# A second ring of weight places for the late modulation, its shares in two stages, and x1 read from PSUM

## The chip, the core and the metric

One core of one Trainium2 chip runs the kernel. The metric is the device time of one execution in microseconds (us); smaller is better. The engines are named as in the profile: PE is TensorE (matrix products; PEld is its weight load), DVE is VectorE, ACT is ScalarE, POOL is GpSimd, and SP is SyncE, whose queue issues nearly all transfers from HBM.

## The reference

One layer of a hybrid diffusion backbone on 256 latent tokens and 256 context tokens of width 2048, all in float32. Cut to what matters here:

```python
sh1, sc1, g1, sh2, sc2, g2 = jnp.split(jax.nn.silu(c) @ w_ada[l] + b_ada[l], 6, axis=-1)
p = modulate(rmsnorm(x, norm_mix[l]), sh1, sc1) @ w_in[l]        # split into the columns of both branches and the gates
y_mla_l = attend_latent(q_l, k_l, v_l, k_c, v_c)                  # latent attention, 8 heads
o_dn_l, _ = dn_bidirectional(lq, lk, lv, lgd, lbeta, s_ctx, True) # gated delta rule, two directions, from the context's state
merged = jax.nn.sigmoid(gate_mla) * (y_mla @ w_o_mla) + jax.nn.sigmoid(gate_dn) * (y_dn @ w_o_dn)
x = x + g1 * (merged @ w_out)                                     # x1
h = modulate(rmsnorm(x, norm_ffn[l]), sh2, sc2)
gate, val = jnp.split(h @ w_up, 2, axis=-1)
x = x + g2 * ((jax.nn.silu(dwconv_centred(gate, conv_w)) * val) @ w_down)
```

## The kernel before, in words

Activations lie with channels on the 128 partitions and the 256 tokens (T) along the row. Every large product is made from two halves: a weight block is loaded in float32 (`raw`, 128x1024, 512 KB), ScalarE casts it to the high half (`whi`, L120), VectorE subtracts to get the low half (`wlo`, L121), and TensorE multiplies both (`mm_hl`, L68): a 128x512 product with the high half, whose two halves of 256 columns hold the activation's high and low part, and a 128x256 product with the low half. One output tile is therefore in one PSUM bank as two halves of 256 columns that still have to be added: `gather` does this with a copy on ScalarE (L513) and an add on VectorE (L514).

`raw` has a ring of NR = 5 places (pool `wr`, tag "raw"); `whi` and `wlo` have NH = 6 each. SP, ACT and VectorE run in the order in which the program is written; TensorE does so in the attention and in the scan, elsewhere a scheduler orders it. A load whose place is still in use holds up what is behind it on SP.

The stages, with where they lie in the profiled span: projections and attention to about 730 us; the scan of the gated delta rule (`scan`, tiles `S`, `r`, `kp`, `yp`, `o`) from about 735, whose gaps on TensorE are filled by other tiles (`e_fill`): gate projections `wgd` (`gtp`, copied to `zx`) and the attention branch's output projection `womla` (`brp`, `ox`, `t1`); the norm of o; the delta branch's projection `wodn`; the output projection `wout` (`ops`, from about 995), whose loop over f makes x1 and its sum of squares; the norm; the FFN (`fps`, 1100 to 1590), whose first four tiles are made k by k while `h2_tile` makes h and H; the down projection (`dps`).

The late modulation is `ada_rest`: the last four of the six modulation vectors (g1, sh2, sc2, g2; one value for each of 128 x 64 channels) are made on VectorE, not on TensorE. 128 loads of 512 KB (`rawa`, L259) are each multiplied by the row of silu(c) (`sch`, 128x1024, reloaded from `Sc` for each half) and summed in one instruction (a "dot", L278, followed by a small read of the sum into `parts`). It is a generator: `ada(c)` adds c to what is owed, and a dot pays 1300. So ADS (in the scan, times the cost the scan reports), the number 1 (a dot for each of the scan's last pieces) and WO (each wout tile) set how many dots stand where. Its loads used the same five places as the weights, and one load was issued ahead of the dot before it. g1 must be done before x1, sh2 and sc2 before the norm's end, g2 before the down projection.

```python
x1[:, f] = yx * adaT[:, f] + xr      # L1387, yx = ops high half + low half
```

Of the kernel before, what the change touches and what calls it, by code (L numbers as in the profile page):

```python
# [8 lines left out]
F32 = mybir.dt.float32  # L9
F32R = mybir.dt.float32r  # L10
AF = mybir.ActivationFunctionType
ALU = mybir.AluOpType
# [4 lines left out]
P = 128  # L17
D = 2048
KD = D // P
T = 256  # L20
# [7 lines left out]
GR = 1024  # L28
GH = 512
NR = 5  # L30
# [6 lines left out]
CB = 3000  # L37
CC = 7000
RE = 1.0
ADS = 0.3  # L40
OD = 8000
OC = 4000
WO = 1500
IK = 7000
NW = 4
SCP = (0, 2, 4, 6)
# [7 lines left out]
def hybrid_block(ctx: ExitStack, tc: tile.TileContext, io, dbg=None):  # L54
    nc = tc.nc
    act, dve, pool, sync = nc.scalar, nc.vector, nc.gpsimd, nc.sync
# [23 lines left out]
    def pool_(name, bufs, side="left"):  # L80
        return tc.tile_pool(name=name, bufs=bufs, side=side, reuse_waits="tile")
# [4 lines left out]
    wr = ctx.enter_context(pool_("wr", 2))  # L86
# [4 lines left out]
    def dump(name, ap):  # L91
        if dbg is not None and name in dbg:
            sync.dma_start(dbg[name], ap)
# [8 lines left out]
    half = const.tile([P, 1], F32, name="half")  # L102
# [26 lines left out]
    def load_w(src):  # L129

        g = []
        for o in range(0, src.shape[1], GR):
            raw = raw_w(src[:, o : min(o + GR, src.shape[1])])
            for i in range(0, raw.shape[1], GH):
                n = min(GH, raw.shape[1] - i)
                hi = wp.tile([P, GH], F32R, tag="whi", name="whi", bufs=NH)[:, :n]
                lo = wp.tile([P, GH], F32R, tag="wlo", name="wlo", bufs=NH)[:, :n]
                split(raw[:, i : i + n], hi, lo)
                g.append((hi, lo))
        return lambda o, m=P: tuple(w[:, o % GH : o % GH + m] for w in g[o // GH])  # L140
# [12 lines left out]
    def mm_hl(ps, M, w, x, first, last):  # L153

        hi, lo = w
        xf = x.rearrange("p a b -> p (a b)")
        if last and not first:
            pe.matmul(ps[:M, :T], lo, x[:, 0, :], start=False, stop=False)
            pe.matmul(ps[:M, :], hi, xf, start=False, stop=True)
        else:  # L160
            pe.matmul(ps[:M, :], hi, xf, start=first, stop=False)
            pe.matmul(ps[:M, :T], lo, x[:, 0, :], start=False, stop=last)
# [88 lines left out]
    adaT = const.tile([P, 64], F32, name="adaT")  # L251

    def ada_rest():


        def load(i):
            w = wr.tile([P, GR], F32, tag="raw", name="rawa", bufs=NR)
            c, n = divmod(i, 32)
            sync.dma_start(w, io["wada2"][c, (n // 16 + c) % 2, n % 16])  # L259
            return w  # L260

        parts = ad.tile([P, 2, 16], F32, name="parts")
        half, ahead = None, load(0)
        for i in range(128):
            c, n = divmod(i, 32)
            h, j = (n // 16 + c) % 2, n % 16
            if h != half:

                for _ in range(1 if i else 0):
                    yield 1300  # L270
                half, sch = h, ad.tile([P, GR], F32, tag="sch", name="sch")
                sync.dma_start(sch, Sc[h])
                for _ in range(3):
                    yield 1300
            w = ahead
            if i < 127:
                ahead = load(i + 1)
            dve.tensor_tensor_reduce(out=w, in0=w, in1=sch, scale=1.0, scalar=0.0, op0=ALU.mult, op1=ALU.add, accum_out=parts[:, h, j : j + 1])  # L278
            if n == 31:
                cs = slice(16 * c, 16 * c + 16)  # L280
                dve.tensor_tensor(out=adaT[:, cs], in0=parts[:, 0], in1=parts[:, 1], op=ALU.add)
                dve.tensor_tensor(out=adaT[:, cs], in0=adaT[:, cs], in1=bada[:, 32 + 16 * c : 48 + 16 * c], op=ALU.add)
                ada.done = c + 1
            yield 1300
# [123 lines left out]
    def load(*what):  # L408
        for kind, n in what:
            d, f = {"w": (wts, load_scale), "s": (shifts, load_shift), "g": (grs, load_first)}[kind]  # L410
            d[n] = f(n)
# [99 lines left out]
    def gather(ps, M, out, scale=None):  # L511

        act.copy(out, ps[:M, T:])  # L513
        dve.tensor_tensor(out=out, in0=ps[:M, :T], in1=out, op=ALU.add)  # L514
# [20 lines left out]
    def proj(src, segs, side=lambda c: None):  # L535
        W = load_w(src)
        pss = [psm.tile([P, 512], F32, tag="mm", name="mmp") for _ in segs]
        for k in range(KD):
            for ps, s in zip(pss, segs):
                mm_hl(ps, P, W(k * P), H[s][:, k], k == 0, k == KD - 1)  # L540
            side(353 * len(segs))
        return pss
# [31 lines left out]
    pl = pg.tile([P, 8, 8], F32, name="plx")  # L574
# [8 lines left out]
    g = pg.tile([P, 8, 8], F32, name="gx")  # L583
# [30 lines left out]
    for st in range(8):  # L614
        B = [pg2.tile([P, 8, 64], F32R, tag=f"B{n}", name="B") for n in range(2)]
        for n in range(2):
            dve.tensor_tensor(out=B[n], in0=mle64.unsqueeze(1).broadcast_to([P, 8, 64]),
                              in1=ghl[:, n, st].unsqueeze(2).broadcast_to([P, 8, 64]), op=ALU.mult)
# [136 lines left out]
    def head_inputs(h, side=lambda c: None):  # L755
        if h < N1:
            xs = [dkx[:, 2 * h], dkx[:, 2 * h + 1]]
        else:
            xs = []
            for w in ("wdk", "wdv"):  # L760
                pss = proj(io[w][h], (0, 1), side)
                x = pb2.tile([P, 2, T], F32, tag="cx", name="cx")
                for s in range(2):
                    gather(pss[s], P, x[:, s])
                xs.append(x)
        ps = proj(io["wdq"][h], (0,), side)[0]
        xq = pb2.tile([P, 1, T], F32, tag="cq", name="cq")
        gather(ps, P, xq[:, 0])
        return xs[0], xs[1], xq

    ada = Side(ada_rest())
    ada.done = 0
    ins = {h: head_inputs(h) for h in (3, 0)}

    def chains(*hs):
# [394 lines left out]

    pT = ctx.enter_context(pool_("pt", 1))
    t1 = pT.tile([P, KD, T], F32, tag="t1", name="t1")
    pD = ctx.enter_context(ExitStack())
    pd = pD.enter_context(pool_("pd", 1))
    pd2 = pD.enter_context(pool_("pd2", 2))
# [173 lines left out]
    for c in scan():  # L1349
        fill(RE * c)  # L1350
        ada(ADS * c)
    pM = ctx.enter_context(ExitStack())
# [10 lines left out]
    pd3 = pD.enter_context(pool_("pd3", 2))  # L1363
# [9 lines left out]
    x1 = pT.tile([P, KD, T], F32, tag="t1", name="x1")  # L1373
# [3 lines left out]
    for f in range(KD):  # L1377
        W = load_w(io["wout"][f])
        ps = psm.tile([P, 512], F32, tag="mm", name="ops")
        for k in range(KD):  # L1380
            mm_hl(ps, P, W(k * P), MG[k], k == 0, k == KD - 1)
        if f % 2 == 0:
            xr = pd3.tile([P, 2, T], F32, tag="xr", name="xr")
            sync.dma_start(xr, io["xT"][:, f : f + 2])
        yx = pd3.tile([P, T], F32, tag="gx", name="yx")
        gather(ps, P, yx)
        dve.scalar_tensor_tensor(out=x1[:, f], in0=yx, scalar=adaT[:, f : f + 1], in1=xr[:, f % 2], op0=ALU.mult, op1=ALU.add)  # L1387
        sq = pd3.tile([P, T], F32, tag="t2", name="x1q")
        act.activation(sq if f else ssq[:, 0], x1[:, f], AF.Square)
        if 0 < f < KD - 1:  # L1390
            dve.tensor_tensor(out=ssq[:, 0], in0=ssq[:, 0], in1=sq, op=ALU.add)
        ada(WO)
    dump("x1", x1)
# [44 lines left out]
    for f in range(NFF):  # L1438
        xs = []
        for w in ("wgate", "wval"):  # L1440
            ps = fps.get((w, f))
            if ps is None:
                W = load_w(io[w][f])
                ps = psm.tile([P, 512], F32, tag="mm", name="fps")
# [5 lines left out]
        gx, vx = xs  # L1450
# [10 lines left out]
    for f in range(KD):  # L1461
        ps = psm.tile([P, 512], F32, tag="mm", name="dps")
# [3 lines left out]
        yx = pf2.tile([P, T], F32, tag="fy", name="yo")  # L1466
# [106 lines left out]
```

## Time and profile before

| | |
|---|---|
| median of three runs | 1839.57 us (1839.47 to 1844.64) |
| profiled execution | 1835.39 us, span 1833.5 us |
| mean granted TensorE clock | 0.992 |
| TensorE busy | 1773.5 us, 97% |
| VectorE busy | 1367.2 us, 75% |
| ScalarE busy | 914.6 us, 50% |
| moved by DMA | 419.72 MB, 229 GB/s in the mean |
| L278 dots | 128, 1221 ns each, VectorE idle 47.1 us before them |

The profiled execution is one run; the median stands 4.2 us above it. Shares of the whole span are means over stages: a stage has to be read by its own stretch. In the fences below, a timeline row is start, duration, engine, line, operation, output and inputs, and in square brackets the idle time before it and what ended it.

### The profile page before, as it was taken

The numbers are of one execution on the slowest core, as the hardware profiler recorded it, in microseconds if no ns is written. First come the engines' busy times: TensorE is split into PE (matmuls) and PEld (weight loads), VectorE is DVE, ScalarE is ACT, GpSimd is POOL, SyncE is SP. The second block draws the span as 40 slices with busy tenths as digits, with TensorE's granted clock in tenths as the row PEclk, the third lists the DMA queues.
The fourth block names the chain that finished last, engine by engine and source line by source line (L and its number), as shares of the span: only waits on it lengthen the run. The fifth ranks groups of instructions, "written<-read, shape, count | busy, mean of one in ns | idle before, by whom it ended". The sixth has DMA issues, their size and how long they took to land.

```text
span 1833.5 us, 33054 instructions
## 1 busy us (share of the span) xinstructions
PE 1773.5 (97%) x12450; PEld 1526.8 (83%) x12450; DVE 1367.2 (75%) x2766; ACT 914.6 (50%) x1868; POOL 45.5 (2%) x48
## 2 busy tenths in 40 slices
PE   7999999999999998999989979999999999999999
PEld 5787887888888887778878868888888888888887
DVE  4787899778787786676779778888777888755554
ACT  3344444444675665333346445555555555544443
POOL 0000001000000000000000000000000000000000
PEclk9999999999999999999999999999999999999999
DMA  9973788765787767887757875777766777766663
GB/s 382 402 299 100 213 238 225 222 202 145 232 258 240 240 210 223 299 269 260 262 169 238 280 246 180 251 220 223 228 191 208 224 221 220 227 196 200 197 198 120
DMA packets 195009, 419.72 MB, mean 229 GB/s; under 512 B 61280, under 2 KB 101344, under 8 KB 192416
## 3 DMA queue, kind: packets, MB, share of 16 engines
q1 hardware_dynamic: 167664, 402.37, 68.6%
q10 hardware_dynamic: 27184, 15.23, 2.7%
q8 instruction: 98, 1.61, 0.3%
q14 instruction: 63, 0.52, 0.1%
HBM read 388.57 MB, written 28.84 MB: 228 GB/s over the span
## 4 chain that ended last, share of the span: by engine, by line
PE 49%; issue 9%; DVE 2%; DMA 2%; ACT 1%; POOL 0%; SPq 0%; POOLq 0%; ACTq 0%; DVEq 0%
PE fps L68 26%; PE dps L68 13%; PE gtp L68 4%; PE brp L68 2%; PE op L68 1%; DVE wlo L121 1%; PE yp L68 1%; DMA Gs<-zx 1%; DMA raw<-in_wgate 1%; DVE r L1264 0%; PE kp L68 0%; ACT whi L120 0%; DMA jit<-Xo 0%; POOL om L172 0%; DMA raw<-in_wgd 0%
## 5 line engine op out<-in xcount | busy, mean ns | idle before, releaser
L121 DVE TENSOR_TENSOR wlo<-raw,whi 128x512 fp32r<-128x512 f32 (+1 forms) x940 | 633.5, 686 | 205.6 <-ACT whi L120 197.3
L120 ACT CAST whi<-raw 128x512 fp32r<-128x512 f32 (+1 forms) x940 | 572.0, 619 | 399.6 <-PE dps L68 114.4
L68 PE MATMUL fps<-H,whi 128*128 128x512 f32 x1376 | 482.4, 399 | 1.8 <-DVE H L1416 1.7
L68 PE MATMUL fps<-H,wlo 128*128 128x256 f32 x1376 | 374.8, 282 | 0.3 <-DVE wlo L121 0.3
L68 PEld LDWEIGHTS fps<-H,whi 128*128 128x128 f32 x1376 | 254.4, 189 | 58.5 <-issue 2.0
L68 PEld LDWEIGHTS fps<-H,wlo 128*128 128x128 f32 x1376 | 259.8, 189 | 8.4 <-DVE wlo L121 0.8
L68 PE MATMUL gtp<-h,whi 128*128 128x512 f32 x640 | 234.4, 402 | 5.1 <-ACT whi L120 5.1
L68 PE MATMUL mmp<-h,whi 128*128 128x512 f32 x640 | 229.0, 400 | 0.0
L68 PE MATMUL dps<-GB,whi 128*128 128x512 f32 x560 | 195.9, 391 | 0.0
L278 DVE CUSTOM_DVE_ANT_0 rawa<-rawa,sch 128x1024 f32<-128x1024 f32 x128 | 156.2, 1221 | 47.1 <-DMA rawa<-in_wada 45.6
L68 PE MATMUL gtp<-h,wlo 128*128 128x256 f32 x640 | 175.6, 285 | 5.5 <-DVE wlo L121 5.5
L68 PE MATMUL mmp<-h,wlo 128*128 128x256 f32 x640 | 176.7, 282 | 0.3 <-DVE wlo L121 0.3
L68 PE MATMUL dps<-GB,wlo 128*128 128x256 f32 x560 | 155.3, 282 | 0.0
L68 PEld LDWEIGHTS gtp<-h,whi 128*128 128x128 f32 x640 | 120.7, 190 | 31.4 <-ACT whi L120 6.3
L68 PEld LDWEIGHTS mmp<-h,whi 128*128 128x128 f32 x640 | 119.1, 188 | 26.1 <-issue 0.4
L68 PEld LDWEIGHTS gtp<-h,wlo 128*128 128x128 f32 x640 | 121.1, 189 | 13.1 <-DVE wlo L121 8.7
L68 PEld LDWEIGHTS mmp<-h,wlo 128*128 128x128 f32 x640 | 120.5, 188 | 3.6 <-DVE wlo L121 0.8
L68 PEld LDWEIGHTS dps<-GB,whi 128*128 128x128 f32 x560 | 105.1, 188 | 21.7
L68 PEld LDWEIGHTS dps<-GB,wlo 128*128 128x128 f32 x560 | 106.0, 189 | 0.6
L68 PE MATMUL fp<-h,gh 128*128 128x256 f32 (+1 forms) x448 | 84.3, 289 | 2.7 <-ACT h L68 1.7
L68 PEld LDWEIGHTS fp<-h,gh 128*128 128x128 f32 (+1 forms) x448 | 68.5, 187 | 7.7 <-issue 4.1
L513 ACT COPY fx<-fps 128x256 f32<-128x256 f32 x86 | 31.9, 374 | 68.2 <-PE fps L68 68.2
(561 smaller groups left out, 2564.6 us busy)
## 6 DMA issues: line engine op xcount, KB each, us to landing
rawa<-in_wada SPq DMA_DIRECT2D x128, 512.0 KB, 4.5
raw<-in_wgate SPq DMA_DIRECT2D x82, 512.0 KB, 4.2
raw<-in_wval SPq DMA_DIRECT2D x82, 512.0 KB, 4.7
raw<-in_wdown SPq DMA_DIRECT2D x80, 512.0 KB, 4.3
wt<-in_wadas SPq DMA_DIRECT2D x16, 1024.0 KB, 10.9
raw<-in_wadab SPq DMA_DIRECT2D x32, 512.0 KB, 9.4
raw<-in_wgm SPq DMA_DIRECT2D x32, 512.0 KB, 5.0
raw<-in_wgd SPq DMA_DIRECT2D x32, 512.0 KB, 6.3
```

Source lines behind the costliest of these rows:

```text
L68: i = f(*a, **k)
L120: act.copy(hi, raw)
L121: dve.tensor_tensor(out=lo, in0=raw, in1=hi, op=ALU.subtract)
L278: dve.tensor_tensor_reduce(out=w, in0=w, in1=sch, scale=1.0, scalar=0.0, op0=ALU.mult, op1=ALU.add, accum_out=parts[:, h, j : j + 1])
L513: act.copy(out, ps[:M, T:])
```

## The change

From the scan on, `rawa` has a ring of its own with two places (pool `ar`), and the load of the dot two further on is issued right behind the dot that frees its place; before the scan, it stays in the weight ring with one load ahead. ADS goes from 0.3 to 0.4 and WO from 1500 to 1000. In the wout loop x1 is made by two VectorE instructions that read the two halves in PSUM; the copy on ScalarE and the tile `yx` are gone there.

```diff
-ADS = 0.3
+ADS = 0.4
-WO = 1500
+WO = 1000
 def load(i):
-    w = wr.tile([P, GR], F32, tag="raw", name="rawa", bufs=NR)
+    pl, tag, n = ada.ring
+    w = pl.tile([P, GR], F32, tag=tag, name="rawa", bufs=n)
...
-half, ahead = None, load(0)
+half, ahead = None, []
...
-    w = ahead
-    if i < 127:
-        ahead = load(i + 1)
+    own = ada.ring[0] is not wr
+    while len(ahead) < 2 - own and i + len(ahead) < 128:
+        ahead.append(load(i + len(ahead)))
+    w = ahead.pop(0)
     dve.tensor_tensor_reduce(out=w, in0=w, in1=sch, ...)
+    if own:
+        while len(ahead) < 2 and i + 1 + len(ahead) < 128:
+            ahead.append(load(i + 1 + len(ahead)))
...
+ada.ring = wr, "raw", NR
...
+ada.ring = ctx.enter_context(pool_("ar", 1)), "rawa", 2     # ahead of the scan
...
-yx = pd3.tile([P, T], F32, tag="gx", name="yx")
-gather(ps, P, yx)
-dve.scalar_tensor_tensor(out=x1[:, f], in0=yx, scalar=adaT[:, f : f + 1], in1=xr[:, f % 2], op0=ALU.mult, op1=ALU.add)
+g = adaT[:, f : f + 1]
+dve.scalar_tensor_tensor(out=x1[:, f], in0=ps[:, T:], scalar=g, in1=xr[:, f % 2], op0=ALU.mult, op1=ALU.add)
+dve.scalar_tensor_tensor(out=x1[:, f], in0=ps[:, :T], scalar=g, in1=x1[:, f], op0=ALU.mult, op1=ALU.add)
```

How many dots stand in each part of the program, counted on VectorE's order:

| part | before | after |
|---|---|---|
| up to the end of attention | 59 | 57 |
| scan | 22 | 32 |
| of these before the first update of S | 3 | 8 |
| norm of o and start of wodn | 0 | 2 |
| wout | 17 | 21 |
| front of the FFN (h2) | 1 | 6 |
| rest of the FFN | 29 | 10 |

Three places of VectorE's order show it. The first is the first step of the scan, from the low half of the weight that the second `brp` needs (9053 before, 9058 after) to the `ox` behind `r`. Before:

```order
L121 TENSOR_TENSOR wlo_9053<-raw_9050,whi_9052 128x512
L121 TENSOR_TENSOR wlo_9057<-raw_9050,whi_9056 128x512
L514 TENSOR_TENSOR zx_9045<-gtp_8992,zx_9045 128x256
L278 ISA rawa_9069,parts_2173<-rawa_9069,sch_8107 128x1024
...
L1264 SCALAR_TENSOR_TENSOR r_9073<-kp_9075,negc_1683,jit_8836 128x128 x4
L1264 SCALAR_TENSOR_TENSOR r_9074<-kp_9076,negc_1683,jit_8836 128x128 x4
L1197 SCALAR_TENSOR_TENSOR ox_9111<-brp_9060,ox_9111 128x256
L1198 SCALAR_TENSOR_TENSOR t1_8820<-gt_8932,ox_9111 128x256
```

After (each dot also issues the small read of `parts`, left out here):

```order
L519 TENSOR_TENSOR zx_9050<-gtp_8997,zx_9050 128x256
L1206 SCALAR_TENSOR_TENSOR t1_8820<-gt_8937,ox_8966 128x256
L280 ISA rawa_8971,parts_2173<-rawa_8971,sch_8107 128x1024
...
L121 TENSOR_TENSOR wlo_9058<-raw_9055,whi_9057 128x512
L121 TENSOR_TENSOR wlo_9062<-raw_9055,whi_9061 128x512
L280 ISA rawa_9075,parts_2173<-rawa_9075,sch_8107 128x1024
...
L280 ISA rawa_9078,parts_2173<-rawa_9078,sch_8107 128x1024
...
L1272 SCALAR_TENSOR_TENSOR r_9084<-kp_9086,negc_1683,jit_8839 128x128 x4
L1272 SCALAR_TENSOR_TENSOR r_9085<-kp_9087,negc_1683,jit_8839 128x128 x4
L1205 SCALAR_TENSOR_TENSOR ox_9122<-brp_9065,ox_9122 128x256
```

The low half stood ahead of zx; now it stands behind zx, t1 and a dot, and two further dots stand between the second low half and r.

The second place is one tile of the wout loop. Before:

```order
L278 ISA rawa_12620,parts_2173<-rawa_12620,sch_10966 128x1024
...
L121 TENSOR_TENSOR wlo_12563<-raw_12560,whi_12562 128x512
L514 TENSOR_TENSOR yx_12485<-ops_12452,yx_12485 128x256
L121 TENSOR_TENSOR wlo_12567<-raw_12560,whi_12566 128x512
L1387 SCALAR_TENSOR_TENSOR x1_11726<-yx_12485,adaT_88,xr_12420 128x256
L121 TENSOR_TENSOR wlo_12573<-raw_12570,whi_12572 128x512
L1391 TENSOR_TENSOR ssq_11727<-ssq_11727,x1q_12489 128x256
L121 TENSOR_TENSOR wlo_12577<-raw_12570,whi_12576 128x512
L278 ISA rawa_12685,parts_2173<-rawa_12685,sch_10966 128x1024
```

After:

```order
L280 ISA rawa_13962,parts_2173<-rawa_13962,sch_10445 128x1024
...
L1394 SCALAR_TENSOR_TENSOR x1_11752<-ops_12510,adaT_88,xr_12543 128x256
L121 TENSOR_TENSOR wlo_12618<-raw_12611,whi_12617 128x512
L1395 SCALAR_TENSOR_TENSOR x1_11752<-ops_12510,adaT_88,x1_11752 128x256
L121 TENSOR_TENSOR wlo_12624<-raw_12621,whi_12623 128x512
L1399 TENSOR_TENSOR ssq_11753<-ssq_11753,x1q_12547 128x256
L121 TENSOR_TENSOR wlo_12628<-raw_12621,whi_12627 128x512
L280 ISA rawa_14086,parts_2173<-rawa_14086,sch_10445 128x1024
...
L121 TENSOR_TENSOR wlo_12677<-raw_12674,whi_12676 128x512
```

The copy's add (L514) and L1387 became L1394 and L1395. A dot comes more often, and the load for the one behind the next is issued when it ends, where before one load was ahead and stood among the weights' loads on SP for one of the five places.

The third place is the front of the FFN, where the h (L1414, after L1422) and H (L1416, after L1424) of the norm are made while TensorE begins on them. Before:

```order
L1416 SCALAR_TENSOR_TENSOR H2_12780<-h2_12833,adaT_88,H2_12780 128x256
L1416 SCALAR_TENSOR_TENSOR H2_12780<-h2_12845,adaT_88,H2_12780 128x256
L1414 SCALAR_TENSOR_TENSOR h2_12881<-x1_11726,a2_12778,b2_12775 128x256
L1414 SCALAR_TENSOR_TENSOR h2_12893<-x1_11726,a2_12778,b2_12775 128x256
L1416 SCALAR_TENSOR_TENSOR H2_12780<-h2_12881,adaT_88,H2_12780 128x256
L1416 SCALAR_TENSOR_TENSOR H2_12780<-h2_12893,adaT_88,H2_12780 128x256
L1414 SCALAR_TENSOR_TENSOR h2_12905<-x1_11726,a2_12778,b2_12775 128x256
L1414 SCALAR_TENSOR_TENSOR h2_12917<-x1_11726,a2_12778,b2_12775 128x256
L121 TENSOR_TENSOR wlo_12872<-raw_12869,whi_12871 128x512
L121 TENSOR_TENSOR wlo_12878<-raw_12875,whi_12877 128x512
```

After:

```order
L1424 SCALAR_TENSOR_TENSOR H2_12759<-h2_12812,adaT_88,H2_12759 128x256
L280 ISA rawa_14703,parts_2173<-rawa_14703,sch_15192 128x1024
...
L1424 SCALAR_TENSOR_TENSOR H2_12759<-h2_12824,adaT_88,H2_12759 128x256
L1422 SCALAR_TENSOR_TENSOR h2_12860<-x1_11752,a2_12757,b2_12754 128x256
L1422 SCALAR_TENSOR_TENSOR h2_12872<-x1_11752,a2_12757,b2_12754 128x256
L280 ISA rawa_14948,parts_2173<-rawa_14948,sch_15192 128x1024
...
L121 TENSOR_TENSOR wlo_12851<-raw_12848,whi_12850 128x512
L121 TENSOR_TENSOR wlo_12857<-raw_12854,whi_12856 128x512
L1424 SCALAR_TENSOR_TENSOR H2_12759<-h2_12860,adaT_88,H2_12759 128x256
L1424 SCALAR_TENSOR_TENSOR H2_12759<-h2_12872,adaT_88,H2_12759 128x256
```

Dots now stand between the h and H of the norm and ahead of the low halves of the first tiles, with `sch` reloaded for the first of them.

## The prediction

> **What bounds the kernel now.** I read the page first, then the table of busy times by stretch, then TensorE's waits inside the stretch where something moves. (For one row per stage, the columns are stretch, its length, busy us of PE, PEld, DVE, ACT and POOL with counts, granted clock, DMA share, GB/s.)
>
> ```profile
> span 1833.5 us, 33054 instructions
> PE 1773.5 (97%) x12450; PEld 1526.8 (83%) x12450; DVE 1367.2 (75%) x2766; ACT 914.6 (50%) x1868; POOL 45.5 (2%) x48
> ...
> 740.00:760.00 20.00, 16.66 (x117) 13.64 (x116) 12.13 (x26) 7.33 (x15) 0.00 (x0) 1.00 0.82 288
> 760.00:940.00 180.00, 169.46 (x1335) 148.06 (x1338) 126.43 (x310) 65.20 (x137) 0.00 (x0) 0.99 0.79 266
> ...
> 960.00:1000.00 40.00, 40.00 (x230) 34.76 (x230) 39.59 (x93) 27.13 (x61) 0.00 (x0) 1.00 0.70 214
> 1000.00:1090.00 90.00, 84.79 (x473) 71.76 (x472) 70.30 (x135) 40.68 (x87) 0.00 (x0) 1.00 0.82 272
> 1090.00:1100.00 10.00, 4.37 (x51) 3.33 (x49) 7.15 (x16) 4.60 (x10) 0.69 (x1) 0.79 0.65 200
> ...
> 1134.00:1590.00 456.00, 455.92 (x2584) 396.52 (x2585) 367.44 (x713) 248.02 (x486) 0.00 (x0) 1.00 0.72 222
> ```
>
> TensorE is the bound. In the FFN (1134 to 1590) it has 0.08 us without work, so VectorE dots taken out of the FFN win nothing there. What can be won or lost lies in TensorE's gaps before it: 5.21 us in the output projection (1000 to 1090), 5.63 us at the norm behind it, 13.9 us in the scan (740 to 940), and one gap at the end of attention. The waits that make these gaps (total us, times, longest):
>
> ```profile
> PE gtp L68 <- DVE wlo L121: 5.5, 9, 1.7
> PE ops L68 <- DVE wlo L121: 5.1, 7, 2.0
> PE gtp L68 <- ACT whi L120: 5.1, 5, 1.6
> PE ss L68 <- ACT x1q L1389: 2.4, 1, 2.4
> PE yps L68 <- DVE PT L121: 2.2, 1, 2.2
> PE brp L68 <- DVE wlo L121: 2.0, 2, 1.8
> ```
>
> Nearly all are weights whose low half VectorE has not made yet.
>
> **Part 1: two dots leave the end of attention.** There the chain that ended last runs through a dot:
>
> ```profile
> 697.27 4.41 DMA rawa<-in_wada
> 701.71 1.23 DVE rawa L278
> ...
> 703.94 1.67 PE yps L68 x8
> ```
>
> The dot stood on VectorE until its load landed, and the transposed probabilities, queued behind it, reached TensorE 2.2 us late. In the new order the last two dots of attention are gone. Term: -2.2 us, bounds -3 (the dot and its wait leave more than this one gap) and 0 (something else is late there).
>
> **Part 2: the output projection.** VectorE's groups there, the landing time of these loads between 690 and 1134 (minimum, median, maximum), and one case of the wait:
>
> ```profile
> L121 DVE TENSOR_TENSOR wlo<-raw,whi 128x512 fp32r<-128x512 f32 x64 | 43.5, 687 | 2.0 <-ACT whi L120 1.5
> L278 DVE CUSTOM_DVE_ANT_0 rawa<-rawa,sch 128x1024 f32<-128x1024 f32 x17 | 20.8, 1224 | 17.6 <-DMA rawa<-in_wada 17.6
> L1387 DVE SCALAR_TENSOR_TENSOR x<-yx,adaT,xr 128x256 f32<-128x256 f32 x15 | 7.2, 481 | 0.1
> L1197 DVE SCALAR_TENSOR_TENSOR ox<-brp,ox 128x256 f32<-128x256 f32 x1 | 0.4, 421 | 0.0
> ...
> DMA to landing us min/median/max: 3.4/5.4/10.5
> ...
> 1079.69 0.33 SPq L259 DMA_DIRECT2D rawa<-in_wada  x1
> ...
> 1084.27 1.22 DVE L278 CUSTOM_DVE_ANT_0 rawa<-rawa,sch 128x1024 f32<-128x1024 f32 x1 [3.06 <-DMA rawa<-in_wada]
> ...
> 1086.16 0.39 PE L68 MATMUL ops<-MA,wlo 128*128 128x256 f32 x1 [1.99 <-DVE wlo L121]
> ```
>
> The load left SP's queue at 1079.69 (it had waited for a place), landed 4.6 us later, VectorE stood 3.06 us, and the low half behind it came 1.99 us late for TensorE. Such waits are 17.6 us on VectorE and 5.1 on TensorE. After the change there are 21 dots instead of 17 and each load is issued behind the dot two before its own. 85.5 us over 21 dots is a dot every 4.07 us, so from the freeing of a place to its use there are 2 x 4.07 - 1.3 = 6.8 us, against a landing of 5.4. VectorE's work grows by 4 x (1.22 + 0.08) = 5.2 us to 75.5 of 85.5, which the 17.6 us of waits cover; were they not gone, TensorE would wait more than now. The five weight places no longer hold dots, so weights too come earlier; on SP a load that waits for its place holds up the weight loads behind it, and in the new order it stands behind a dot that is long over. The transfers rise from 272 GB/s to (90 x 0.272 + 4 x 0.524 MB) / 85.5 us = 311 GB/s: the cover may be thin for the loads that take up to 10.5 us. Term: -4.5, bounds -5.2 (all of the gap) and -2.
>
> The x1 edit in this loop costs VectorE nothing that counts: before 0.42 (the add, row in part 3) + 0.48 us a tile; now two instructions with one PSUM operand, for which the nearest rows are 421 (L1197, also from PSUM) and 481 ns, together about 0.90 again (bounds -0.06 and +0.1 a tile, 16 tiles, in VectorE's spare time). ScalarE loses 16 copies and is not the bound. On this form the Trainium skill ("VectorE: DVE Perf Modes", section "Why PSUM operands drop a tier") says a PSUM operand holds an fp32 operation at the single rate; L1197 at 421 ns is such an operation and no slower than the rest of its size, so the sum stays.
>
> **Part 3: the norm behind it.** Only here does the x1 edit lie on the path:
>
> ```profile
> 1092.05 0.40 PE L68 MATMUL ops<-MB,whi 128*128 128x512 f32 x1
> ...
> 1093.67 0.36 ACT L513 COPY yx<-ops 128x256 f32<-128x256 f32 x1
> ...
> 1094.41 0.42 DVE L514 TENSOR_TENSOR yx<-ops,yx 128x256 f32<-128x256 f32 x1
> ...
> 1095.91 0.39 PE L68 MATMUL ss<-ones,x1q 128*32 128x1 f32 x16 [2.44 <-ACT x1q L1389]
> ```
>
> From the last matmul's end (1092.45) to the sum of squares are 3.46 us. The copy stood behind weight casts on ScalarE and the add behind low halves on VectorE. Without them: 0.42 + 0.48 + 0.42 (square) and about 0.1 at each hand-over make 1.6, and up to 0.7 if a low half is running. Term -1.7, bounds -2.1 and 0.
>
> **Part 4: the first step of the scan takes eight dots instead of three.** Rows of before:
>
> ```profile
> 741.39 0.39 PE L68 MATMUL brp<-YM,whi 128*128 128x512 f32 x1
> ...
> 742.00 0.42 DVE L514 TENSOR_TENSOR zx<-gtp,zx 128x256 f32<-128x256 f32 x1 [1.60 <-ACT zx L513]
> 742.34 1.22 DVE L278 CUSTOM_DVE_ANT_0 rawa<-rawa,sch 128x1024 f32<-128x1024 f32 x1
> ...
> 744.03 2.16 DVE L1264 SCALAR_TENSOR_TENSOR r<-kp,negc,jit 128x128 f32<-128x128 f32 x8 [0.47 <-PE kp L68]
> ...
> 748.46 0.38 PE L68 MATMUL gtp<-h,wlo 128*128 128x256 f32 x1 [0.52 <-DVE wlo L121]
> ...
> 754.70 0.50 PE L68 MATMUL gtp<-h,whi 128*128 128x512 f32 x1 [1.61 <-ACT whi L120]
> ...
> 754.03 2.40 ACT L120 CAST whi<-raw 128x512 fp32r<-128x512 f32 x4 [0.32 <-DMA raw<-in_wgd]
> ```
>
> TensorE began the branch projection (brp) at 741.39 since its weight's low half had been made before zx. In the new order zx, t1 and dot 8971 stand ahead of that low half, and zx needs the tile before brp on TensorE, as it did at 742.00. So: zx ends 742.4, t1 742.8, dot 744.0, low half 744.7: brp starts about 2.8 us late. Then two more dots (9075, 9078) stand ahead of r. Dot 9078's place is freed by dot 8971 at 744.0; with a landing of 4.6 it runs until 749.9, r (2.16) until 752.0, ox, dot 9081 and t1 until 753.9, and the gate weight's low half is there at 754.6 where it was at 748.46: 6.1 us late. From there before lost 1.61 us on a cast that waited for its transfer, which is absorbed now: 4.5. Term +4.6; bounds +1.5 (loads in 3.4 us, more absorbed) and +10.5 (loads in 10.5 us).
>
> **Part 5: the rest of the scan** gets five dots more (22 before, 32 after, in all), 6.5 us on a VectorE that has 53 us free in 180; weights have their five places to themselves, and some of the gtp and brp waits above (12.6 us in all) go back to late transfers such as the one at 754.03. Term -1.0, bounds -3 and +3. One dot lies between the last adds of o: +0.6 (0 to 1.2). Two dots come into the output projection of the DeltaNet branch (wodn), where VectorE is as full as TensorE (39.59 of 40 us): 2 x 1.3 = 2.6 if nothing gives, 0 if the weights' lead covers it; I take half, +1.3.
>
> **Part 6: the front of the FFN** gets six dots for one while h and H of the new norm are made:
>
> ```profile
> L121 DVE TENSOR_TENSOR wlo<-raw,whi 128x512 fp32r<-128x512 f32 x12 | 7.8, 689 | 4.3 <-ACT whi L120 4.3
> ```
>
> VectorE idles 4.3 us there, which hides two or three of the five added dots; the others stand ahead of low halves made just in time. 5 x 1.15 (back to back an operation hides about 0.08 of the next) = 5.75 at most, 0 at least. The reload of the 512 KB of scales, which stood inside the FFN, now falls here too, on SP ahead of two of these loads and of the weights behind them; if it lands late the fourth H waits with the dot, within the same bounds. Term +2.5. The ten dots that the FFN keeps come closer together in its first tiles: +0.3 (0 to 2). The 19 taken away there win 0.
>
> **Sum** (us): -2.2 + 4.6 - 1.0 + 0.6 + 1.3 - 4.5 - 1.7 + 2.5 + 0.3 = -0.1. The profiled execution (1835.39 us, 4.2 under the median of 1839.57) would stand at 1835.3; on the median's scale 1839.5.
>
> **The clock.** After a gap of 2.5 us at 724 the records show
>
> ```profile
> 726.00:728.00 2.00, 1.55 (x10) 1.58 (x11) 1.00 (x1) 2.00 (x4) 0.00 (x0) 0.79 0.91 289
> 728.00:730.00 2.00, 2.00 (x10) 1.84 (x10) 2.00 (x3) 0.61 (x2) 0.00 (x0) 0.50 1.04 395
> 730.00:732.00 2.00, 2.00 (x12) 1.73 (x11) 0.82 (x2) 1.15 (x3) 0.00 (x0) 0.86 1.06 252
> ```
>
> so 2 x (0.21 + 0.50 + 0.14) = 1.7 us of work were lost to a lower clock, while the two gaps of the first scan step (0.98 and 1.61 us) left it at 1.00. A step of scan with one gap of 3 to 5 us may lose the same: 1839.5 + 1.7 = 1841.2. The Trainium skill ("TensorE: Matmul & The Clock Gate", section "What's actually happening") has the half rate begin only after an idle window of about 3.4 us that runs freely. By that rule the 2.8 us gap would cost nothing and the longer one something; the trace shows it after 2.5 us already, so I give the drop one chance in two and leave it inside "no change".
>
> **The rivals.** *Faster* (0.32): step one and the FFN's front lose little. For it: the first scan step stalled on weights anyway (0.98, 0.52, 1.61), and dots leave the weight ring, so later weights land earlier; against it: the order of the low half behind zx is fixed. It gives -2.2 + 1.5 - 3 + 0.6 - 5.2 - 2.1 + 1 = -9.4: 1830. *Slower* (0.21): the scan's dots wait for their own loads in VectorE's fixed order. The place is dot 9078 and its like, 2.8 us of work behind the freeing of their place; the price is the landing time less that lead, with r and the recurrence behind it. At 10.5 us part 4 gives 10.5 and part 5 +1: the sum is 7.8, 1847.4. It decides from a part 4 of about 10, a landing near 10 us. Against it stands the median of 5.4. *The second place brings nothing in the output projection* because the transfers, at 311 GB/s, land later (part of "no change"): term 0 instead of -4.5, 1844.0; for it, the share of 0.82 already; against it, 395 GB/s in a row above.
>
> **How the numbers follow.** No change 0.47 (with the clock and the transfer case), faster 0.32, slower 0.21; 0.3% (5.5 us, about what the spread 1839.47 to 1844.64 can tell) bounds them. The range 1830 to 1848 leaves out about half of the faster case and less of the slower, 2 in 10 together.
>
> **What would show it.** Right: TensorE's wait of ops for wlo near zero and VectorE's wait for rawa under 4 us between 995 and 1093 by before's times; yps no longer waiting for PT; a gap of 2 to 3 us at the first brp of the scan and one before the next gtp; a norm gap near 4 us; the FFN from its second tile on the same to 0.5 us. Wrong: no gap at that brp (part 4), a scan whose dots stand for their loads for more than 8 us in sum (the slower case), an FFN front that is longer by over 4 us, or a projection that is as long as before.

## The result and the profile after

The changed kernel takes 1848.7 us in the median (1847.07 to 1850.27, six runs) against 1839.26 us (1835.01 to 1844.64): ratio 1.0054, 95% interval 1.004 to 1.0067. It is slower by about 10 us. The forecast was 1839.5 (1830 to 1848), with no change as the likeliest case; the result lies above the end of the range.

One correction first. The section on the kernel says that VectorE runs in the order in which the program is written. That holds only for instructions that are pinned. The rest, the dots among them, a scheduler moves as far forward as their data and their places allow: the dots that stand in the FFN's front in the new order are written in the FFN's first tiles. The order shown there is what ran; the reason given for it was wrong, and it matters below.

The same stretches of the profile after (columns as before; stages lie some 10 us later from the scan on):

```profile
740.00:760.00 20.00, 12.60 (x65) 9.96 (x66) 12.59 (x28) 3.08 (x6) 0.00 (x0) 0.77 0.92 312
760.00:940.00 180.00, 168.73 (x1238) 147.33 (x1238) 128.16 (x309) 64.05 (x132) 0.00 (x0) 0.99 0.79 270
...
1000.00:1090.00 90.00, 90.00 (x515) 78.61 (x514) 79.23 (x155) 43.66 (x84) 0.00 (x0) 1.00 0.87 293
1090.00:1100.00 10.00, 7.67 (x51) 5.90 (x53) 10.00 (x20) 3.54 (x8) 0.00 (x0) 1.00 0.72 231
1100.00:1134.00 34.00, 22.85 (x142) 19.02 (x143) 27.63 (x58) 15.15 (x31) 0.70 (x1) 0.85 0.73 227
1134.00:1590.00 456.00, 455.60 (x2581) 395.73 (x2580) 351.98 (x685) 249.70 (x489) 0.00 (x0) 1.00 0.65 200
```

TensorE has no gap left in wout, but in the row that holds most of the scan's first step its busy time falls by a quarter (16.66 to 12.60 us), and the stretch behind wout, with the norm and the FFN's front, is emptier than before. TensorE's longest waits between 690 and 1134, for the list shown of before:

```profile
PE gtp L68 <- ACT whi L120: 7.2, 5, 4.5
PE fps L68 <- DVE H L1424: 5.8, 4, 1.7
PE brp L68 <- ACT whi L120: 5.0, 2, 3.1
PE ss L68 <- ACT x1q L1397: 4.3, 1, 4.3
```

By stage, measured between the starts of the same TensorE tiles in the profiles (first yp, first yp that reads r, last kp, first ops, last ops, sum of squares, last fps), in us against the first profile of before; the last rows are the same two kernels profiled again:

| kernel | ahead of the scan | scan, step one | rest of scan | o norm, wodn | wout | norm | FFN |
|---|---|---|---|---|---|---|---|
| forecast | -2.2 | +4.6 | -1.0 | +1.9 | -4.5 | -1.7 | +2.8 |
| changed | -1.4 | +10.3 | +0.5 | +2.6 | -6.3 | +3.0 | +3.6 |
| changed, again | +1.2 | +9.7 | +0.2 | +2.6 | -3.8 | +2.4 | +4.2 |
| before, again | +4.8 | +1.1 | +0.2 | +0.5 | -1.0 | -0.1 | +0.1 |

The first column is no measure: one program's profiles lie 5 us apart there. The others repeat to about 1 us, wout to 2.5.

**Step one of the scan.** TensorE does the same work in 24.65 us before (first row) and 35.00 us after (second row), in windows that begin and end at the marks:

```profile
726.45:751.10 24.65, 23.16 (x160) 19.94 (x161) 12.89 (x25) 9.29 (x19) 0.00 (x0) 0.93 0.79 261
```

```profile
725.00:760.00 35.00, 26.30 (x161) 21.77 (x162) 19.92 (x38) 9.82 (x20) 0.00 (x0) 0.87 0.85 281
```

Of these 10.35 us, 8.70 - 1.49 = 7.2 are gaps, and 26.30 - 23.16 = 3.1 are the same matmuls at a lower clock. What came late is in SP's queue. Before:

```profile
733.32 0.38 SPq L126 DMA_DIRECT2D raw<-in_womla  x1
733.79 0.38 SPq L259 DMA_DIRECT2D rawa<-in_wada  x1
...
735.97 0.41 SPq L126 DMA_DIRECT2D raw<-in_wgd  x1
```

After, on SP and then on ScalarE and TensorE:

```profile
735.76 0.38 SPq L126 DMA_DIRECT2D raw<-in_womla  x1
736.23 6.21 SPq L260 DMA_DIRECT2D rawa<-in_wada  x2
...
745.14 0.33 SPq L260 DMA_DIRECT2D rawa<-in_wada  x1
...
746.04 0.38 SPq L126 DMA_DIRECT2D raw<-in_wgd  x1
...
753.72 1.14 ACT L120 CAST whi<-raw 128x512 fp32r<-128x512 f32 x2 [3.38 <-DMA raw<-in_wgd]
...
742.69 0.49 PE L68 MATMUL brp<-YM,whi 128*128 128x512 f32 x1 [3.15 <-ACT whi L120]
...
754.39 0.80 PE L68 MATMUL gtp<-h,whi 128*128 128x512 f32 x1 [4.47 <-ACT whi L120]
```

The pair of rawa issues lasts 6.21 us since the second waits on SP until dot 8971 has freed its place. Behind it stand the scan's next K, then another rawa that waits for the next dot, and behind that the gate weight (wgd), which leaves at 746.04 where it left at 735.97. TensorE then stood 4.47 us for its cast.

The 3.15 us at brp are another matter. The branch weight (womla) left SP 10.8 us after the first yp, where it had left after 6.9. No load that waited for a dot stood ahead of it: SP stood at the tiles that wait until the gates, stored from ScalarE's queue (`Gs`), have landed (725 to 745, before and after):

```profile
SPq L1187 <- DMA Gs<-zx: 2.5, 1, 2.5
...
SPq L1234 <- DMA Gs<-zx: 4.8, 1, 4.8
```

The store landed 5.8 us after its issue, before 2.8. In the changed kernel the new ring's two empty places let two dot loads leave at the start of the step, ahead of it; in the six profiles that have them there on SP the store took 4.6 to 7.3 us, in the seven without them 1.9 to 3.9 (experiment 7 apart). That these loads slow it is read from this comparison; no run isolates it.

**Norm and FFN's front.** VectorE at the end of wout; the last ops matmul began at 1097.7:

```profile
1099.77 1.22 DVE L280 CUSTOM_DVE_ANT_0 rawa<-rawa,sch 128x1024 f32<-128x1024 f32 x1
...
1100.91 1.28 DVE L121 TENSOR_TENSOR wlo<-raw,whi 128x512 fp32r<-128x512 f32 x2
1102.12 0.47 DVE L1394 SCALAR_TENSOR_TENSOR x<-ops,adaT,xr 128x256 f32<-128x256 f32 x1
1102.63 0.48 DVE L1395 SCALAR_TENSOR_TENSOR x<-ops,adaT,x 128x256 f32<-128x256 f32 x1
...
1104.47 0.40 PE L68 MATMUL ss<-ones,x1q 128*32 128x1 f32 x16 [4.26 <-ACT x1q L1397]
```

VectorE is full (10.00 of 10 us above), 4 us behind TensorE, and a dot that is written in the FFN stands ahead of the last x1.

### The profile page after: what moved, and what is told of

The parts are those of the page before. It is cut to its first block, busy times and chain, and to the rows that moved or that the text cites. A ratio compares the mean times of both kernels' runs of the same rounds, so it can differ in the third digit from the quotient of the medians.

```text
span 1845.6 us, 33098 instructions
## 1 busy us (share of the span) xinstructions
PE 1778.8 (96%) x12450; PEld 1530.8 (83%) x12450; DVE 1371.3 (74%) x2766; ACT 912.2 (49%) x1852; POOL 45.5 (2%) x48
## 3 DMA queue, kind: packets, MB, share of 16 engines
q8 instruction: 98, 1.61, 0.3%
## 4 chain that ended last, share of the span: by engine, by line
PE 74%; issue 10%; DMA 7%; DVE 5%; ACT 2%; POOL 1%; SPq 0%; POOLq 0%; ACTq 0%; DVEq 0%
PE fps L68 26%; PE dps L68 13%; PE mmp L68 12%; PE gtp L68 7%; PE fp L68 4%; DMA rawa<-in_wada 2%; PE brp L68 2%; DVE wlo L121 1%; DMA raw<-in_wadab 1%; PE op L68 1%; PE amp L68 1%; DMA raw<-in_wgd 1%; DVE rawa L280 1%; ACT whi L120 1%; PE tp L68 1%
```

## The experiments

Ratios are those to the kernel before, measured beside it, with 95% intervals. A gain in us is worked out from the ratio; the difference of the medians departs from it by up to 2.6 us. The stage figures come from one profile each.

**1. The x1 edit alone.**

```diff
-yx = pd3.tile(...); gather(ps, P, yx)
-dve.scalar_tensor_tensor(out=x1[:, f], in0=yx, scalar=..., in1=xr[:, f % 2], ...)
+dve.scalar_tensor_tensor(out=x1[:, f], in0=ps[:, T:], scalar=g, in1=xr[:, f % 2], ...)
+dve.scalar_tensor_tensor(out=x1[:, f], in0=ps[:, :T], scalar=g, in1=x1[:, f], ...)
```

> The kernel before with the x1 edit alone; the order of the dots is unchanged. Theory A (the loss of the changed kernel comes from the dots and their loads, not from x1): the copy and the add leave the chain at the norm, the gap between the last ops and the sum of squares falls from 3.46 to 1.5 to 2.5 us, ratio 0.9985 to 1.000. Theory C (the x1 edit itself makes the norm later, because VectorE now does both reads): that gap grows as in the changed kernel, to 5 us or more, ratio 1.001 to 1.003.

1834.14 us, ratio 0.9975 (0.9963 to 0.9987): faster by 4.6 us (the medians are 2.9 apart), more than either theory said, though the interval reaches theory A's. Theory C falls. Theory A's place was wrong: wout is 3.4 us shorter (of which the second profile of before explains 1.0 as spread), the norm is not shorter (+0.5): low halves of the FFN now stand ahead of the last x1 there, one of which waits 0.8 us for its cast. VectorE's chain of an add that waited for ScalarE's copy is gone from each tile, and TensorE's wait of ops for wlo falls from 5.1 and 3.6 (two profiles) to

```profile
PE ops L68 <- DVE wlo L121: 2.8, 4, 1.1
```

**2. The ring alone** (the old shares 0.3 and 1500, the old x1).

```diff
-ADS = 0.4
+ADS = 0.3
-WO = 1000
+WO = 1500
```

(against the changed kernel, with x1 as before)

> Own ring of two places with the old shares (0.3 and 1500) and the old x1. The order has 6 dots in the scan's first step (before 3, changed 8), 22 in wout and 6 in the FFN's front, so the ring alone moves dots forward. Theory A (the ring is the cause: its loads wait on SP ahead of the scan's transfers and gate weights, and dots are moved ahead of the norm): step one loses 5 to 10 us, wout wins 4 to 6, the norm and the FFN's front lose 5 to 8; ratio 1.003 to 1.006. Rival (the larger share in the scan is the cause): step one loses at most 3 us, ratio 0.997 to 1.001.

1844.1 us, ratio 1.0034 (1.0021 to 1.0047), as theory A said. Step one +4.2, between the two theories, o and wodn +2.2, wout -4.5, norm +3.3, FFN +3.9. The losses behind the scan are those of the changed kernel: the ring alone, without the new shares, brings them.

**3. The dots held in place.**

```diff
-dve.tensor_tensor_reduce(out=w, in0=w, in1=sch, ...)
+(odve if own else dve).tensor_tensor_reduce(out=w, in0=w, in1=sch, ...)   # odve: kept in written order
```

> The changed kernel with its dots, from the scan on, held to the place at which they are written on VectorE: 7 dots around the scan's first step, 12 in wout, none in the FFN's front, 29 in the FFN. Theory A: the FFN's front wins back 3 to 4 us and the norm 4 to 5; step one of the scan still loses 5 to 10 us, since the gate weight's load still stands on SP behind two loads that wait for a dot. Ratio to before 0.999 to 1.003. Rival B (dots ahead of the low half and of r on VectorE make step one's loss): here the low half of the branch weight stands ahead of zx again, and step one loses under 4 us; ratio 0.996 to 0.999.

1847.73 us, ratio 1.0048 (1.0035 to 1.0061): slower than expected. Norm -1.9, FFN +0.4, wout -7.4, as theory A said. Step one +8.8, although the low half stands ahead of zx again: rival B falls as it was put. What no theory had: the rest of the scan +10.1. SP's waits in the scan (735 to 930) for a dot's place, before, changed and here, and behind them TensorE's longest here:

```profile
SPq L259 <- DVE parts L278: 10.1, 2, 9.3
...
SPq L260 <- DVE parts L280: 46.2, 13, 8.1
...
SPq L260 <- DVE parts L68: 61.0, 17, 9.0
...
PE gtp L68 <- ACT whi L120: 16.7, 5, 6.3
```

**4. The same, with the loads issued from GpSimd's queue.**

```diff
-sync.dma_start(w, io["wada2"][...])
+(sync if pl is wr else pool).dma_start(w, io["wada2"][...])
```

> The same as the kernel with the dots held, but the loads of the own ring are issued from GpSimd's queue; the order on VectorE and TensorE is the same but for one dot's two rows. Theory A: the gate weights and the scan's tiles no longer stand behind waiting loads on SP; step one loses 5 us or more less than with the dots held alone, ratio to before 0.994 to 0.998. Rival B (VectorE's order): within 2 us of the kernel with the dots held. A further rival: issuing from GpSimd costs its own time and the dots wait longer.

1824.21 us, ratio 0.9916 (0.9895 to 0.9936): better than theory A said, 15 us better than before and 24 better than experiment 3, with the same order on TensorE and (but for two rows) on VectorE. That is the queue. TensorE has no wait of gtp for a cast left in the scan. Most of the gain is in the rest of the scan (-7.6 for +10.1); step one loses 5.4 where it lost 8.8, so it wins 3.4, not the 5 expected. In the scan TensorE and VectorE now wait:

```profile
PE gtp L68 <- DVE wlo L121: 7.1, 2, 5.0
PE yp L68 <- DVE r L1272: 4.1, 1, 4.1
...
DVE rawa L68 <- DMA rawa<-in_wada: 21.7, 8, 5.2
```

The 5.0 is in step one, the rest of the first two rows behind it. Dots that wait for their own loads (21.7 us, in experiment 3 1.2) hold up low halves and r. So rival B is half right: with the queue cleared, VectorE's order shows in step one, at about the size that part 4 gave it.

**5. The shares alone** (old ring, old x1).

```diff
-ADS = 0.3
+ADS = 0.4
-WO = 1500
+WO = 1000
```

> The kernel before with the new shares alone (0.4 in the scan, 1000 in wout), old ring, old x1: 5 dots in the scan's first step, 29 in the scan, 11 in wout, 2 in the FFN's front. Theory A (own ring with its loads on SP makes the loss): wout wins 2 to 3 us from six dots fewer, the scan changes by less than 3 us; ratio 0.997 to 1.000. Rival (the larger share in the scan makes the loss): the scan loses 4 us or more; ratio 1.001 to 1.004.

1839.17 us, ratio 1.0009 (0.9992 to 1.0027): no difference that can be told from none. Step one +4.5, as the rival said, and wout -3.4, as theory A said: the larger share does cost step one, and wout's fewer dots pay for it. In step one TensorE stands 4.54 us at 756.27 for the cast of a gate weight, so a late gate weight needs no own ring.

**6. The ring only from wout on.**

```diff
-ada.ring = ctx.enter_context(pool_("ar", 1)), "rawa", 2      # ahead of the scan
+ar = ctx.enter_context(pool_("ar", 1)), "rawa", 2            # same place in memory
...
 while ada.done < 1:
     ada(1)
+ada.ring = ar
```

> The changed kernel, but its own ring begins only ahead of the wout loop; in the scan the loads use the weight ring as before, with 5 dots in the first step and 29 in the scan, then 3 around wodn, 21 in wout and 5 in the FFN's front. Theory A: the scan's first step loses under 3 us (changed kernel 10); wout, the norm and the FFN's front stay as in the changed kernel (-6, +3, +3.6). Ratio 0.999 to 1.002. Rival B (dots in the scan are too many): the scan still loses 7 us or more, ratio 1.003 to 1.006.

1846.69 us, ratio 1.0054 (1.0034 to 1.0074): missed. Step one is +2.8 as expected, the norm +3.8 and the FFN +2.1 as in the changed kernel. But wout gains only 3.7 (changed 6.3), and at the end of attention TensorE again waits 2.42 us for the probabilities behind a dot, which the changed kernel did not. What was saved in step one was lost there and in wout; the remaining part of the difference is in the column that a single profile can't measure, and stays open.

**7. The changed kernel on GpSimd's queue, dots free to move.** The edit is that of experiment 4 on the changed kernel.

> The changed kernel with the loads of its own ring issued from GpSimd's queue and the dots free to move: the order then has them early, 8 in the first step of the scan, 31 in its rest, 23 in wout and none behind. Theory A: no weight waits behind a load for a dot, and no dot stands in the FFN's front (-3.6); the dots' waits for their own loads move to VectorE. Ratio 0.992 to 1.000. Rival B (VectorE's order makes the loss): more dots in the scan lose more, ratio 1.004 or above.

1856.05 us, ratio 1.0104 (1.0079 to 1.0129): the slowest, against theory A as it was put and as rival B said. Freed of SP, the scheduler puts all dots ahead of the FFN, and in the scan they wait for their own loads on VectorE:

```profile
PE brp L68 <- DVE wlo L121: 8.9, 1, 8.9
...
DVE rawa L280 <- DMA rawa<-in_wada: 37.9, 15, 5.7
```

Step one loses 15.5, wout 5.2, the stretch of o and wodn 8.1. The queue alone is no cure; the dots must also not be moved forward.

**8. GpSimd's queue, dots held, fewer of them.**

```diff
-ADS = 0.4
+ADS = 0.3
-WO = 1000
+WO = 1400
```

(against experiment 4)

> Dots held to their written place, loads from GpSimd's queue, x1 from PSUM, with the old share of 0.3 in the scan (4 dots in the first step, 23 in all), 1400 in wout (16 dots) and 32 in the FFN. In the kernel with 0.4 TensorE still lost about 9 us in the scan's first step to a low half and to r behind dots that waited for their loads. Theory A with that addition: the first step wins back 4 to 8 us, wout loses at most 1; ratio to before 0.987 to 0.991. Rival: the first step's loss is the late gate weights, whatever the dots; ratio 0.991 to 0.993.

1817.13 us, ratio 0.9891 (0.9867 to 0.9916): 20 us faster than before, the best kernel here, as theory A said. Step one -1.0, rest of the scan -10.9, wout -7.4, norm -1.9, FFN +1.6. (The 9 us named in the expectation are not all in step one: 5.0 of them are.) TensorE's waits for weights in the scan fall from 12.6 us before to

```profile
PE gtp L68 <- DVE wlo L121: 3.0, 4, 2.4
...
PE gtp L68 <- ACT whi L120: 1.2, 1, 1.2
```

**9. The changed kernel with its dots held from wout on.**

```diff
-dve.tensor_tensor_reduce(out=w, in0=w, in1=sch, ...)
+(odve if ada.held else dve).tensor_tensor_reduce(out=w, in0=w, in1=sch, ...)
...
 while ada.done < 1:
     ada(1)
+ada.held = True
```

> The changed kernel with its dots held to their written place from the wout loop on (12 in wout, none between the norm of o and wout, none in the FFN's front, 29 in the FFN); the scan is as in the changed kernel. If dots moved forward by the scheduler make the losses behind the scan: o and wodn win back 2 us, wout keeps -5 to -7, the norm goes from +3 to -2, the FFN's front from +3.6 to under +1: about 9 us in all, ratio to before 0.999 to 1.002. If instead VectorE's low halves made ahead for the FFN hold up x1, the norm and the front stay and the ratio is 1.004 or above.

1833.55 us, ratio 0.9973 (0.9958 to 0.9987): faster than before, by 5 us, and better than expected. Norm -1.9, FFN +0.4, o and wodn +0.5, wout -7.4; the scan still loses (step one +9.3, rest +3.2). Holding the 41 dots from wout on, and nothing else, turns the changed kernel's sign. That dots moved forward made the losses behind the scan is shown.

**10 and 11. Both kernels again.**

> The kernel before, unchanged, profiled a second time: how far two profiles of one program differ by stage. Expected from the x1 edit alone, which has the same order up to wout: up to 4 us ahead of the scan, under 1 us in the scan and behind it.

> The changed kernel, unchanged, profiled a second time. Expected: the scan's first step again 8 to 11 us longer than before, the norm 3, the FFN's front 3 to 4; ahead of the scan anything within 4 us.

1841.13 and 1851.69 us; their stages stand in the table above. The spread is a little larger than expected: before differs by 4.8 ahead of the scan and by 1.1 in step one, and the changed kernel by 2.5 in wout; its norm is +2.4 and its FFN +4.2.

**12. Experiment 8 with the loads on SP.** The edit undoes that of experiment 4.

> The same as the kernel with fewer dots and loads from GpSimd's queue (0.3, 1400, dots held, x1 from PSUM), but the loads of the own ring are issued from SP again, as in the changed kernel: the fourth of two queues by two shares. If SP's queue makes most of the scan's loss, SP again waits 25 us or more in the scan for a dot, TensorE waits for casts of late gate weights, and the kernel stands 8 us or more above the one on GpSimd's queue: ratio to before 0.994 to 1.002. If the number of dots makes it, the two are within 3 us: ratio 0.988 to 0.991.

1842.11 us, ratio 1.0014 (0.9999 to 1.0029), as expected of the queue: step one +8.3 and the rest of the scan +9.7, where experiment 8 has -1.0 and -10.9. With experiments 3, 4 and 8:

| dots held | loads on SP | on GpSimd |
|---|---|---|
| 0.4 and 1000 | 1.0048 | 0.9916 |
| 0.3 and 1400 | 1.0014 | 0.9891 |

The queue is worth 0.012 to 0.013 (22 to 24 us) at either share, the share 0.003. In the scan SP waits, and TensorE again for the casts of gate weights:

```profile
SPq L260 <- DVE parts L68: 69.1, 16, 10.1
...
PE gtp L68 <- ACT whi L120: 13.9, 6, 4.1
```

## Why the prediction was wrong

**Parts 4 and 5 (the scan) are the largest miss:** together +3.6 forecast, +10.8 and +9.9 measured, nearly all of it in step one, near the upper bound of 10.5 but not for its reason. (The 1.61 us that part 4 takes off, at 754.70, lie just behind step one by the table's marks; the sum of both parts does not depend on that.) The working followed VectorE alone: dots ahead of the low half and of r. The step that failed is a sentence of part 2: that in the new order a load "stands behind a dot that is long over". With two places and the load issued right behind the dot that frees one, that dot is the newest, and SP, which runs ahead of VectorE, stops at it: 46.2 us in the scan where it had been 10.1. Part 4 itself counted only transfers, and no queue. The order in which SP issues follows from the program, and the working shows none of it: it has the gate weight behind those loads, and the 4.47 us gap ended on that weight's cast.

The price is not the 46.2 us: SP stood before as well, 23.5 us at dot loads and 15.9 at weights until a low half had freed a place. Experiments 3, 4, 8 and 12 give it: with the dots held, the queue alone moves the time by 22 to 24 us and step one by 3.4 (larger share) or 9.3 (smaller). Most of the 22 to 24 lies in the rest of the scan, where the changed kernel lost only 0.5; how much of its own 10 us is the queue is read from its trace and not isolated, since experiment 7, which changes the queue alone, lets the dots move as well.

VectorE's order, the forecast's reason, is a second cause, and it ran nearly in time with the first. In the changed kernel VectorE stood only 0.58 us before the branch weight's low half and 1.80 us before the gate weight's, each time for the cast, and r began 23.1 us into the step, where the working has 23.5. With SP cleared, experiment 4 still loses 5.4 there. So the signs that the prediction named, a gap of 2 to 3 us at that brp and one before the next gtp, came out (3.15 and 4.47), but both ended on a late weight: in part that is luck.

**The clock** was left out of the sum as one chance in two at 1.7 us. It cost 3.1 in step one on balance (23.16 to 26.30 us of busy time for the same matmuls). The 1.7 that before loses at 726 to 732 is in its 23.16, and the changed kernel has 1.00 in these rows, so its own two drops cost about 3.1 + 1.7 = 4.8, an estimate:

```profile
744.00:746.00 2.00, 2.00 (x10) 1.46 (x10) 1.11 (x2) 0.00 (x0) 0.00 (x0) 0.50 0.97 387
746.00:748.00 2.00, 2.00 (x29) 2.00 (x28) 1.07 (x1) 0.00 (x0) 0.00 (x0) 0.69 1.02 395
...
754.00:756.00 2.00, 1.61 (x4) 1.07 (x5) 1.42 (x3) 0.86 (x2) 0.00 (x0) 0.52 0.72 155
756.00:758.00 2.00, 2.00 (x8) 1.71 (x7) 1.46 (x4) 0.00 (x0) 0.00 (x0) 0.50 0.75 205
758.00:760.00 2.00, 2.00 (x9) 1.71 (x8) 0.00 (x0) 0.00 (x0) 0.00 (x0) 0.50 0.94 344
```

The rows at 744 to 748 follow the 3.15 us gap, those at 754 to 760 the 4.47 us gap. The Trainium skill ("TensorE: Matmul & The Clock Gate", section "What's actually happening") has the half rate begin after an idle window of about 3.4 us that runs freely, which a gap of 4.47 us can hold and one of 3.15 us cannot. The trace agrees for the longer gap and not for the shorter one. In the kernel before the drop came after 2.5 us at 724 and after 1.76 us at 787.90 too (0.65 and 0.50 in the two rows from 788), while the 1.61 us at 754.70 left the clock at 1.00.

**Part 3 (the norm) has the wrong sign:** -1.7 forecast, +3.0 and +2.4 measured. The copy did leave the chain. But the term took VectorE to be at hand when ops ended ("up to 0.7 if a low half is running"), while 21 dots had made it full and a dot of the FFN, with low halves, stood ahead of the last x1. The order of VectorE, on which the dots were counted, has that dot there. With the dots held the term is -1.9 (experiments 3, 4, 8, 9, 12), the size forecast.

**Part 2 (wout)** came out near its size: -4.5 forecast (bounds -5.2 and -2), -6.3 and -3.8 in two profiles, and TensorE's wait of ops for wlo at 0.4 and 2.1. Its mechanism held in part. The x1 edit was costed at nothing there; alone it gave 4.6 us in the whole and -3.4 here, the ring alone -4.5, both together -6.3 and -3.8, so they seem to win the same gaps. Its two instructions took 478 and 479 ns, 0.96 us a tile where 0.90 was forecast, inside the bounds. Dots waited 9.9 us, not under 4. The lead was there, but SP's queue took part of it: the loads left up to 4.1 us after their place was free. In the last rows below, a place was free when the dot of 1059.44 ended, at 1060.66, and its load left at 1064.76, behind two weight loads of which the second waited for a place; it landed just before 1072.26, and the dot had waited 2.32 us:

```profile
L280 DVE CUSTOM_DVE_ANT_0 rawa<-rawa,sch 128x1024 f32<-128x1024 f32 x21 | 25.6, 1221 | 10.0 <-DMA rawa<-in_wada 9.9
L1395 DVE SCALAR_TENSOR_TENSOR x<-ops,adaT,x 128x256 f32<-128x256 f32 x15 | 7.2, 479 | 0.1
L1394 DVE SCALAR_TENSOR_TENSOR x<-ops,adaT,xr 128x256 f32<-128x256 f32 x15 | 7.2, 478 | 0.0
...
DMA to landing us min/median/max: 3.6/5.8/7.5
...
1062.30 2.41 SPq L126 DMA_DIRECT2D raw<-in_wout  x2
1064.76 0.42 SPq L260 DMA_DIRECT2D rawa<-in_wada  x1
...
1072.26 1.23 DVE L280 CUSTOM_DVE_ANT_0 rawa<-rawa,sch 128x1024 f32<-128x1024 f32 x1 [2.32 <-DMA rawa<-in_wada]
```

**The rest of part 5, and part 6,** hold: o and wodn +2.6 (forecast +1.9), the FFN with its front +3.6 and +4.2 (+2.8), TensorE in the FFN as full as before with 19 dots fewer; 9 shows that both losses come from dots moved forward. **Part 1** went the way forecast (TensorE no longer waits for PT at the end of attention, after 2.2 before), but its size can't be read from single profiles.

**The rivals.** The slower rival, at 1847.4, lay near the result and had the right place. Its mechanism, dots that wait for their own loads on VectorE, was not what decided: they waited 2.7 us in the scan, so that its number came near is luck. That wait is what slows experiment 7 (37.9 us). The queue was not among the ways in which step one could lose, so the chance of 0.21 left it out.

## What to carry to other kernels

A ring of its own takes a stream's loads out of the other ring, but not out of the queue: a load issued right behind the instruction that frees its place stops an in-order queue at that instruction, and everything issued behind it pays. Give such a stream a queue that carries nothing urgent, as experiments 4 and 8 do; issuing each load one step after its place is free may do as well and was not tried, nor were held dots in the old ring. And when a scheduler orders the engines, a resource that limited a filler's work also limited how far forward it was put: after freeing it, pin the filler away from the places where its engine is the one waited for, and read every queue's order, not only that of the engine on which the work is done.

## What had not been expected of the hardware

Issuing these 512 KB loads from GpSimd cost 0.54 us of GpSimd's time each in the scan of experiment 4, and they landed in 7.0 us in the median (3.7 to 9.9) where SP's had landed in 4.5 in experiment 3 and in 5.8 before: slower, and still better than experiment 3 by 24 us, with no weight behind them on that queue. Whether the issuing engine or the fuller traffic makes the landing longer is not shown.

```profile
740.16 0.54 POOL L260 DMA_DIRECT2D rawa<-in_wada  x1 [21.43 <-DVE parts L68]
...
DMA to landing us min/median/max: 3.7/7.0/9.9
```
